# The order of TensorE's work in the FFN phases: written out from the second turned chunk on, with two edits at the first and the last chunks

## The chip, the cores and the metric

The kernel runs on one core of a Trainium2 chip. The metric is the device time of one execution in microseconds, a median of several runs. A profiled execution gives the rows below; times in them are counted from the start of its span. TensorE (PE) multiplies, VectorE (DVE) and ScalarE (ACT) work beside it, GpSimd (POOL) does little here, SyncE (SP) issues nearly all DMAs. Each engine takes its instructions in the order of its own queue and waits at semaphores for others.

## The reference

Two layers of a streaming encoder over 256 tokens of 1024 values. Each layer has a half-step FFN, a mixer (four heads of differential attention beside four mLSTM heads) and a second half-step FFN, each between two RMS norms:

```python
def _swiglu(h, w_in, w_out):
    gate, up = jnp.split(h @ w_in, 2, axis=-1)
    return (jax.nn.silu(gate) * up) @ w_out
...
for l in range(DEPTH):
    g = norm_gains[l]
    h = _swiglu(_rmsnorm(x, g[0]), ffn_w_in[l, 0], ffn_w_out[l, 0])
    x = x + 0.5 * _rmsnorm(h, g[1])
    ...
    x = x + _rmsnorm(h, g[3])
    h = _swiglu(_rmsnorm(x, g[4]), ffn_w_in[l, 1], ffn_w_out[l, 1])
    x = x + 0.5 * _rmsnorm(h, g[5])
```

D_FF is 2816, in float32. The change is in the FFN alone; the mixer's code is untouched.

## The kernel before

**Phases and chunks.** Six phases run one after the other: FFN, mixer, FFN, FFN, mixer, FFN, numbered 0 to 5. An FFN is cut into 11 chunks of 256 hidden columns. A chunk needs two weight pieces of 1 MB for its gate and up columns and a third for its rows of the out matrix.

**Weights.** `piece` (L274, L280) has SyncE load a piece into `wr` (three buffers); per half of it ScalarE makes the high part `wh` by a cast (L287) and VectorE the low part `wl` by a subtraction (L288, a "split" in what follows). A product in full precision is three matmuls: high by high, high by low, low by high (`mm3`, L400 to L402). The buffers of `wl` and `wh` come back when the last matmul that reads them is done, and a split into a buffer waits for that matmul.

**Straight and turned chunks.** In a straight chunk the tokens are the stationary operand: per token block one bank, 24 products, then silu, product and two transposes on TensorE (L536). A turned chunk has the weights stationary (`in_turned`, L603): 32 matmuls of 512 columns with the high parts (L609) and 32 of 256 columns with the low parts (L614), into four banks, two of the pool `pin` and two of the pool `ptr`, of two banks each. So each chunk takes the banks of the chunk before it. A bank is emptied in `ffn_block` (L560): ScalarE copies one half (L567), VectorE adds the other to it (L568, the last reader of the bank), multiplies by the token scales (L569), then silu, product (L572), and the parts `hh` (ScalarE, L545) and `hl` (VectorE, L546) for the out products.

**Out products.** `out_part` multiplies the hidden block of an earlier chunk by its out rows into four banks `bk`, 12 matmuls per token block. They wait in a list `pend` and are taken two chunks late; the last ones follow the last chunk.

**What sets the order.** The kernel is written as one program; a scheduler distributes it to the engines and orders each engine's queue by a simulated run, with what was written earlier first among what is ready. Inside a `manual_schedule` region the named engine keeps the written order. In `run` (L486) TensorE enters such a region at the step "ending", when the last chunk's in matrices are done, and leaves it at "running" in the next FFN; so the mixers and the starts of the FFNs are in written order, chunks 2 to 10 are not. VectorE, ScalarE and SyncE are always ordered by the scheduler.

The names in what follows are the tiles' own: `pin`, `ptr`, `bk` are banks, `both` the normalised tokens (high and low parts), `su` the emptied banks, `c` a table of constants.

Of the kernel before, what the change touches and what calls it, by code (L numbers as in the profile page):

```python
# [24 lines left out]
P = 128  # L25
D = 1024
S = 256
NT = S // P
L = 2
DFF = 2816  # L30
NC_FF = DFF // 256
# [2 lines left out]
EPS = 1e-6  # L34
BIG = -1.0e30
DEFER = 3
TURN = 2
AHEAD = 2
AT = (0, 2, 6, 6, 7, 22, 24, 24, 24, 24, 36, 40, 24, 46, 34, 50, 43, 52, 52, 57, 61, 60, 61, 67, 67, 69, 71, 78, 74, 74, 78, 84)
FIRST = """W6 V3 T000 T001 A000 A001 B000 B001 W1 V1 T002 T003 H00 L00 A002 A003 B002 B003 W1 V1 M000 H01 L01  # L40
# [90 lines left out]
class _Trunk:  # L131
# [354 lines left out]
    def run(self, phases):  # L486
        xT, r, last = [], [], []

        def enter(t, ph):
            xT.append(self.prenorm(t, ph))  # L490
            last.append(self.last)

        region = contextlib.ExitStack()
        post = []
        for ph in range(phases):
            half = ph % 3 != 1
            now = (xT, r)
            seen = 0
            self.turns = [[], [], [], [], last[:1], post] if ph else []
            for step in (self.ffn if half else self.mixer)(now, ph):  # L500
                if step == "second":
                    enter(1, ph)
                    r.append(self.rstd(1))
                    self.turns = [last[1:]] * 6
                elif step == "running":
                    region.close()
                elif step == "middle":
                    if ph == 0:
                        self.constants_mix()
                elif step == "ending":  # L510
                    region.enter_context(self.tc.manual_schedule(engines={mybir.EngineType.PE}))
                elif step == "next":
                    if ph + 1 < phases:
                        xT, r, last = [], [], []
                        enter(0, ph + 1)
                else:
                    post = [self.postnorm(seen, step[1], step[2], half, ph + 1 == phases)]
                    seen += 1
                    if seen == NT and ph + 1 < phases:
                        r.append(self.rstd(0))  # L520
        region.close()
# [66 lines left out]
    def ffn(self, pre, gi_post):  # L588
        xT, r = pre

        def in_piece(t, kh, pin, w):
            xh, xl = xT[t][kh]
            for k in range(4):
                self.mm3(pin, xh[:, k, :], xl[:, k, :], *self.cols(w, k),
                         start=kh == 0 and k == 0, stop=kh == 1 and k == 3)
# [4 lines left out]
                    self.mm3(po[t][hf], *h[t][k], *self.cols(wo, 2 * k + hf),  # L600
                             start=c == 0 and k == 0, stop=c == NC_FF - 1 and k == 1)

        def in_turned(banks, w, both):  # L603

            blocks = [(banks[j][i], slice(i * 256 + j * P, i * 256 + j * P + P)) for j in range(2) for i in range(2)]
            for kh in range(2):
                for b, c in blocks:
                    for k in range(4):
                        self.nc.tensor.matmul(b, self.cols(w[kh], k)[0][:, c], both[kh][:, k].rearrange("p i t -> p (i t)"),  # L609
                                              start=kh == 0 and k == 0, stop=False, skip_group_check=True)  # L610
            for b, c in blocks:
                for kh in range(2):
                    for k in range(4):
                        self.nc.tensor.matmul(b[:, 0:NT * P], self.cols(w[kh], k)[1][:, c], both[kh][:, k, 0:NT].rearrange("p i t -> p (i t)"),  # L614
                                              start=False, stop=kh == 1 and k == 3, skip_group_check=True)

        po, pend = None, []
        if not xT:

            xT += [[], []]  # L620
            pins = [self.bank_bk() for _ in range(NT)]
# [10 lines left out]
            begin = 1  # L632
# [29 lines left out]
        for c in range(begin, NC_FF):  # L662
            ws = [self.piece(), self.piece()]
            pend.append((c - 1, h, self.piece()))
            if c == 3:
                g = self.load_gpost(gi_post)
                yield "middle"
            if c < TURN:
                pins = [self.bank_pin() for _ in range(NT)]
                for kh in range(2):  # L670
                    for t in range(NT):
                        in_piece(t, kh, pins[t], ws[kh])
                h = [self.ffn_evac(pins[t], r[t]) for t in range(NT)]
            else:
                if c == TURN:
                    rows, both = self.token_scales(r), list(self.both)
                banks = [[self.bank_pin() for _ in range(2)], [self.bank_tr() for _ in range(2)]]
                in_turned(banks, ws, both)
                if c == NC_FF - 1:
                    break  # L680
                h = self.ffn_turned(banks, rows, c > NC_FF - DEFER - 1)
            if len(pend) == DEFER - 1 or po is None:
                if po is None:
                    po = [[self.bank_bk() for _ in range(2)] for _ in range(NT)]
                cc, hc, wo = pend.pop(0)
                for t in range(NT):
                    out_part(cc, t, hc, wo)

        yield "ending"
        pend.append((c, self.ffn_turned(banks, rows, True), self.piece()))  # L690
        for p in pend:
            out_part(p[0], 0, *p[1:])
# [562 lines left out]
```

## Time and profile before

| | us |
|---|---|
| median of three runs | 978.14 |
| the runs | 980.10, 976.82, 978.14 |
| the profiled execution | 980.56 |
| its span | 978.7 |
| TensorE busy | 967.0 (99% of the span) |
| VectorE busy | 692.4 (71%) |
| ScalarE busy | 564.4 (58%) |

The granted clock of TensorE over the span is 0.997 of full speed. Busy time is what an engine spent in instructions; TensorE's matmuls overlap by some tenths of a microsecond, so the distance between two starts tells more than the length of one. A run of 16 matmuls in one row gives the spacing by the start of the row behind it.

### The profile page before, as it was taken

Reading aid. Unit: us, or ns where it says so; the run is one execution under the profiler, and the core shown is the slowest. Engines: PE = TensorE matmul, PEld = TensorE weight load, DVE = VectorE, ACT = ScalarE, POOL = GpSimd, SP = SyncE. Lnnn points to the kernel's source line nnn. Section 1 sums busy time; section 2 is a strip of 40 time slices with the busy share of each in tenths; the row PEclk is TensorE's granted clock in tenths of the full one; section 3 lists DMA queues with packets and bytes.
Section 4 is the critical chain, followed back from the end, with each engine's and each line's share of the span. In section 5 each row is a group of like instructions: output and inputs, shape, how many; then the busy total and the mean of one; then the engine's idle time right before and its main releaser. Section 6 shows DMA issues by size and latency. Waiting matters only on the chain.

```text
span 978.7 us, 13455 instructions
## 1 busy us (share of the span) xinstructions
PE 967.0 (99%) x5067; PEld 820.0 (84%) x5067; DVE 692.4 (71%) x1177; ACT 564.4 (58%) x1041; POOL 30.0 (3%) x55
## 2 busy tenths in 40 slices
PE   9999999899999999999999999999999999999997
PEld 7888888788788888888788888888888888888886
DVE  7686667589867766857686684767898586676764
ACT  7755455378765555555375554555779475545542
POOL 2000000000020000000000000000001100000000
PEclk9999999999999999999999999999999999999999
DMA  8954546235352835464445545462464346545421
GB/s 321 337 195 169 209 159 230 115 130 196 128 215 87 310 142 214 173 215 156 189 167 204 210 173 213 156 233 90 169 234 150 111 180 232 211 170 218 152 107 44
DMA packets 27648, 178.94 MB, mean 183 GB/s; under 512 B 3034, under 2 KB 4186, under 8 KB 6846
## 3 DMA queue, kind: packets, MB, share of 16 engines
q1 hardware_dynamic: 27006, 177.46, 49.2%
q8 instruction: 40, 0.66, 0.3%
q10 hardware_dynamic: 576, 0.61, 0.2%
q14 instruction: 26, 0.21, 0.1%
HBM read 177.01 MB, written 1.05 MB: 182 GB/s over the span
## 4 chain that ended last, share of the span: by engine, by line
PE 88%; DVE 5%; DMA 4%; ACT 2%; issue 1%; DVEq 0%; POOLq 0%; ACTq 0%; SPq 0%
PE pin L609 11%; PE ptr L609 11%; PE bk L400 8%; PE bk L401 8%; PE bk L402 8%; PE pin L400 7%; PE pin L402 7%; PE pin L401 7%; PE pin L614 6%; PE ptr L614 6%; DMA wr<-in_w_dram 4%; DVE wl L288 3%; ACT wh L287 1%; PE ptr L877 1%; PE ptr L426 1%
## 5 line engine op out<-in xcount | busy, mean ns | idle before, releaser
L288 DVE TENSOR_TENSOR wl<-wr,wh 128x1024 fp32r<-128x1024 f32 x324 | 385.2, 1219 | 92.0 <-ACT wh L287 42.9
L287 ACT ACTIVATE wh<-wr 128x1024 fp32r<-128x1024 f32 x324 | 328.6, 1052 | 134.4 <-PE bk L402 38.4
L400 PE MATMUL bk<-wh,hh 128*128 128x512 f32 x352 | 138.7, 394 | 4.7 <-ACT hh L545 4.7
L609 PE MATMUL pin<-both,wh 128*128 128x512 f32 x576 | 142.5, 390 | 0.0
L609 PE MATMUL ptr<-both,wh 128*128 128x512 f32 x576 | 140.9, 389 | 0.0
L401 PE MATMUL bk<-wl,hh 128*128 128x512 f32 x352 | 138.2, 393 | 0.0
L402 PE MATMUL bk<-wh,hl 128*128 128x512 f32 x352 | 136.9, 391 | 0.0
L609 PEld LDWEIGHTS ptr<-both,wh 128*128 128x128 f32 x576 | 107.7, 188 | 22.2
L609 PEld LDWEIGHTS pin<-both,wh 128*128 128x128 f32 x576 | 107.3, 188 | 21.8
L400 PE MATMUL pin<-wh,both 128*128 128x512 f32 x304 | 122.4, 404 | 0.0
L401 PE MATMUL pin<-wl,both 128*128 128x512 f32 x304 | 119.1, 392 | 0.0
L402 PE MATMUL pin<-wh,both 128*128 128x512 f32 x304 | 118.8, 391 | 0.0
L568 DVE TENSOR_TENSOR su<-pin,su 128x256 f32<-128x256 f32 x72 | 29.2, 420 | 100.9 <-ACT su L567 100.3
L400 PEld LDWEIGHTS bk<-wh,hh 128*128 128x128 f32 x352 | 66.6, 189 | 18.4 <-ACT hh L545 5.8
L545 ACT ACTIVATE hh<-su 128x256 fp32r<-128x256 f32 (+1 forms) x96 | 32.2, 358 | 82.9 <-DVE su L572 60.3
L402 PEld LDWEIGHTS bk<-wh,hl 128*128 128x128 f32 x352 | 66.5, 189 | 14.5 <-DVE hl L546 0.5
L614 PEld LDWEIGHTS pin<-both,wl 128*128 128x128 f32 x576 | 75.5, 191 | 3.8
L614 PE MATMUL pin<-both,wl 128*128 128x256 f32 x576 | 77.1, 283 | 0.0
L401 PEld LDWEIGHTS bk<-wl,hh 128*128 128x128 f32 x352 | 66.6, 189 | 12.1
L614 PE MATMUL ptr<-both,wl 128*128 128x256 f32 x576 | 74.9, 283 | 0.0
L614 PEld LDWEIGHTS ptr<-both,wl 128*128 128x128 f32 x576 | 72.2, 192 | 0.8
L402 PEld LDWEIGHTS pin<-wh,both 128*128 128x128 f32 x304 | 57.1, 188 | 12.4
(202 smaller groups left out, 1000.5 us busy)
## 6 DMA issues: line engine op xcount, KB each, us to landing
wr<-in_w_dram SPq DMA_DIRECT2D x162, 1024.0 KB, 4.9
gpost<-in_gpost_dram SPq DMA_DIRECT2D x6, 512.0 KB, 6.0
wr<-in_w_dram SPq DMA_DIRECT2D x2, 512.0 KB, 6.0
wr<-in_w_dram SPq DMA_DIRECT2D x3, 256.0 KB, 4.2
x<-in_x_dram SPq DMA_DIRECT2D x3, 256.0 KB, 4.7
out_dram<-x SPq DMA_DIRECT2D x2, 256.0 KB, 2.2
x<-in_x_dram SPq DMA_DIRECT2D x2, 128.0 KB, 2.7
wr<-in_w_dram ACTq DMA_DIRECT2D x1, 256.0 KB, 3.2
```

The source lines that it names most:

```text
L287: ia = nc.scalar.activation(hi, raw[:, j], AF.Copy)
L288: iv = nc.vector.tensor_tensor(lo, raw[:, j], hi.bitcast(F32), op=ALU.subtract)
L400: mm(ps, xh, wh, start=start, stop=False)
L401: mm(ps, xh, wl, start=False, stop=False)
L402: mm(ps, xl, wh, start=False, stop=stop)
L426: nc.tensor.transpose(ptr[:, k, :], x[:, (4 * hf + k) * P:(4 * hf + k + 1) * P], self.ident)
L545: self.nc.scalar.activation(hh, h, AF.Copy)
L568: nc.vector.tensor_tensor(su[:, i], bank[i][:, 0:n], su[:, i], op=ALU.add)
L609: self.nc.tensor.matmul(b, self.cols(w[kh], k)[0][:, c], both[kh][:, k].rearrange("p i t -> p (i t)"), start=kh == 0 and k == 0, stop=Fals ...
L614: self.nc.tensor.matmul(b[:, 0:NT * P], self.cols(w[kh], k)[1][:, c], both[kh][:, k, 0:NT].rearrange("p i t -> p (i t)"), start=False, sto ...
L877: self.T(ptr[:, b, :], a[:, b * P:(b + 1) * P], self.tr.ident)
```

## The change

It does three things, all in the FFN.

First, TensorE's written order now begins at a step "steady", at the chunk after the first turned one (chunk 2 of phase 0, chunk 3 of the other FFNs), instead of at "ending". The out products are put in the program one by one for that: the first block of the first pending chunk after the first turned chunk, the second after the next, and from then on whole ones.

Second, chunk 1 of phase 0, straight before, is turned (TURN is gone). The row of token scales is made at the first turned chunk.

Third, `in_turned` takes the last chunk in three groups: the first weight half, high and low parts, for all four banks; then the second half for the two pin banks; then for the two ptr banks. Other chunks keep their order: all high parts, then all low parts, bank by bank.

```diff
--- before.py
+++ after.py
@@ -34,7 +34,6 @@
 EPS = 1e-6
 BIG = -1.0e30
 DEFER = 3
-TURN = 2
 AHEAD = 2
...
@@ -507,7 +506,7 @@
                 elif step == "middle":
                     if ph == 0:
                         self.constants_mix()
-                elif step == "ending":
+                elif step == "steady":
                     region.enter_context(self.tc.manual_schedule(engines={mybir.EngineType.PE}))
                 elif step == "next":
                     if ph + 1 < phases:
@@ -600,19 +599,21 @@
                     self.mm3(po[t][hf], *h[t][k], *self.cols(wo, 2 * k + hf),
                              start=c == 0 and k == 0, stop=c == NC_FF - 1 and k == 1)
 
-        def in_turned(banks, w, both):
+        def in_turned(banks, w, both, last):
+
 
             blocks = [(banks[j][i], slice(i * 256 + j * P, i * 256 + j * P + P)) for j in range(2) for i in range(2)]
-            for kh in range(2):
-                for b, c in blocks:
-                    for k in range(4):
-                        self.nc.tensor.matmul(b, self.cols(w[kh], k)[0][:, c], both[kh][:, k].rearrange("p i t -> p (i t)"),
-                                              start=kh == 0 and k == 0, stop=False, skip_group_check=True)
-            for b, c in blocks:
-                for kh in range(2):
-                    for k in range(4):
-                        self.nc.tensor.matmul(b[:, 0:NT * P], self.cols(w[kh], k)[1][:, c], both[kh][:, k, 0:NT].rearrange("p i t -> p (i t)"),
-                                              start=False, stop=kh == 1 and k == 3, skip_group_check=True)
+            for group, khs in ((blocks, (0,)), (blocks[:2], (1,)), (blocks[2:], (1,))) if last else ((blocks, (0, 1)),):
+                for kh in khs:
+                    for b, c in group:
+                        for k in range(4):
+                            self.nc.tensor.matmul(b, self.cols(w[kh], k)[0][:, c], both[kh][:, k].rearrange("p i t -> p (i t)"),
+                                                  start=kh == 0 and k == 0, stop=False, skip_group_check=True)
+                for b, c in group:
+                    for kh in khs:
+                        for k in range(4):
+                            self.nc.tensor.matmul(b[:, 0:NT * P], self.cols(w[kh], k)[1][:, c], both[kh][:, k, 0:NT].rearrange("p i t -> p (i t)"),
+                                                  start=False, stop=kh == 1 and k == 3, skip_group_check=True)
 
         po, pend = None, []
         if not xT:
@@ -665,28 +666,23 @@
             if c == 3:
                 g = self.load_gpost(gi_post)
                 yield "middle"
-            if c < TURN:
-                pins = [self.bank_pin() for _ in range(NT)]
-                for kh in range(2):
-                    for t in range(NT):
-                        in_piece(t, kh, pins[t], ws[kh])
-                h = [self.ffn_evac(pins[t], r[t]) for t in range(NT)]
-            else:
-                if c == TURN:
-                    rows, both = self.token_scales(r), list(self.both)
-                banks = [[self.bank_pin() for _ in range(2)], [self.bank_tr() for _ in range(2)]]
-                in_turned(banks, ws, both)
-                if c == NC_FF - 1:
-                    break
-                h = self.ffn_turned(banks, rows, c > NC_FF - DEFER - 1)
-            if len(pend) == DEFER - 1 or po is None:
-                if po is None:
-                    po = [[self.bank_bk() for _ in range(2)] for _ in range(NT)]
-                cc, hc, wo = pend.pop(0)
-                for t in range(NT):
-                    out_part(cc, t, hc, wo)
-
-        yield "ending"
+            if c == begin + 1:
+                yield "steady"
+            if c == begin:
+                rows, both = self.token_scales(r), list(self.both)
+            banks = [[self.bank_pin() for _ in range(2)], [self.bank_tr() for _ in range(2)]]
+            in_turned(banks, ws, both, c == NC_FF - 1)
+            if c == NC_FF - 1:
+                break
+            h = self.ffn_turned(banks, rows, c > NC_FF - DEFER - 1)
+            if po is None:
+                po = [[self.bank_bk() for _ in range(2)] for _ in range(NT)]
+
+            for t in ((0,) if c == begin else (1,) if c == begin + 1 else range(NT)):
+                out_part(pend[0][0], t, *pend[0][1:])
+            if c > begin:
+                pend.pop(0)
+
         pend.append((c, self.ffn_turned(banks, rows, True), self.piece()))
         for p in pend:
             out_part(p[0], 0, *p[1:])
```

The lines of the changed kernel are one less than before's down to in_turned (the add that empties a bank is L567, the split L287), and high and low matmuls of a turned chunk are L610 and L615.

**TensorE, from one turned chunk to the next, in phase 0.** Before, from the last low matmuls of chunk 2 into its second ptr bank (ptr_475) on; pin_649 and pin_650 are the banks of chunk 3, wh the high parts of its pieces:

```order
L614 MATMUL ptr_475<-both_187,wl_1_453 128x256 x2
L609 MATMUL pin_649<-both_129,wh_0_569 128x512 x2
L609 MATMUL pin_649<-both_129,wh_1_573 128x512 x2
L609 MATMUL pin_650<-both_129,wh_0_569 128x512 x2
L609 MATMUL pin_650<-both_129,wh_1_573 128x512 x2
L609 MATMUL pin_649<-both_187,wh_0_579 128x512 x2
L609 MATMUL pin_649<-both_187,wh_1_583 128x512 x2
L609 MATMUL pin_650<-both_187,wh_0_579 128x512 x2
L609 MATMUL pin_650<-both_187,wh_1_583 128x512 x2
```

After these rows come the low matmuls of the two pin banks and 12 out products, and then the ptr banks of chunk 3 (ptr_651, ptr_652). In the changed kernel, at the same step from chunk 1 to chunk 2, from the last low matmuls into ptr_345 on; ptr_486 and ptr_487 are the ptr banks of chunk 2, and ptr_487 is the place of ptr_345:

```order
L615 MATMUL ptr_345<-both_187,wl_1_323 128x256 x2
L610 MATMUL ptr_486<-both_129,wh_0_455 128x512 x2
L610 MATMUL ptr_486<-both_129,wh_1_459 128x512 x2
L610 MATMUL ptr_487<-both_129,wh_0_455 128x512 x2
L610 MATMUL ptr_487<-both_129,wh_1_459 128x512 x2
```

The 16 high and 16 low matmuls of the pin banks and the 12 out products no longer stand between a ptr bank's last matmul and the first of its successor; four matmuls do.

**VectorE at the same place of the changed kernel.** ptr_344 and ptr_345 are chunk 1's ptr banks, wl_0_474 to wl_1_596 the splits of two later pieces:

```order
L567 TENSOR_TENSOR su_425<-ptr_344,su_425 128x256
L568 TENSOR_TENSOR su_425<-su_425,rows_340 128x256
L545 TENSOR_TENSOR hl_411<-su_414,hh_410 128x256
L287 TENSOR_TENSOR wl_0_474<-wr_472,wh_0_475 128x1024
L287 TENSOR_TENSOR wl_1_478<-wr_472,wh_1_479 128x1024
L287 TENSOR_TENSOR wl_0_592<-wr_590,wh_0_593 128x1024
L287 TENSOR_TENSOR wl_1_596<-wr_590,wh_1_597 128x1024
L567 TENSOR_TENSOR su_425<-ptr_345,su_425 128x256
```

Each of the four splits waits for low matmuls into ptr_345, the add of ptr_345 behind them for the last of these. In the kernel before, four splits stand ahead of the two ptr adds of chunk 2 in the same way, so this order on VectorE has stayed.

**VectorE at the end of phase 0.** Before; su_1767 comes from the pin banks of the last chunk, su_1780 from its ptr banks (1695, 1696):

```order
L568 TENSOR_TENSOR su_1767<-pin_1693,su_1767 128x256
L568 TENSOR_TENSOR su_1767<-pin_1694,su_1767 128x256
L569 TENSOR_TENSOR su_1767<-su_1767,rows_470 128x256
L288 TENSOR_TENSOR wl_0_1946<-wr_1944,wh_0_1947 128x1024
L569 TENSOR_TENSOR su_1767<-su_1767,rows_470 128x256
L568 TENSOR_TENSOR su_1780<-ptr_1695,su_1780 128x256
L288 TENSOR_TENSOR wl_0_1936<-wr_1934,wh_0_1937 128x1024
L288 TENSOR_TENSOR wl_1_1940<-wr_1934,wh_1_1941 128x1024
L288 TENSOR_TENSOR wl_1_1950<-wr_1944,wh_1_1951 128x1024
L568 TENSOR_TENSOR su_1780<-ptr_1696,su_1780 128x256
L572 TENSOR_TENSOR su_1767<-su_1767 128x256
L569 TENSOR_TENSOR su_1780<-su_1780,rows_470 128x256 x2
```

And in the changed kernel, where su_1789 comes from the pin banks (1717, 1718), su_1802 from the ptr banks (1719, 1720):

```order
L287 TENSOR_TENSOR wl_0_1958<-wr_1956,wh_0_1959 128x1024
L287 TENSOR_TENSOR wl_0_1968<-wr_1966,wh_0_1969 128x1024
L567 TENSOR_TENSOR su_1789<-pin_1717,su_1789 128x256
L567 TENSOR_TENSOR su_1789<-pin_1718,su_1789 128x256
L568 TENSOR_TENSOR su_1789<-su_1789,rows_340 128x256 x2
L287 TENSOR_TENSOR wl_1_1962<-wr_1956,wh_1_1963 128x1024
L571 TENSOR_TENSOR su_1789<-su_1789 128x256
L287 TENSOR_TENSOR wl_1_1972<-wr_1966,wh_1_1973 128x1024
L567 TENSOR_TENSOR su_1802<-ptr_1719,su_1802 128x256
L567 TENSOR_TENSOR su_1802<-ptr_1720,su_1802 128x256
L545 TENSOR_TENSOR hl_1786<-su_1789,hh_1785 128x128
L568 TENSOR_TENSOR su_1802<-su_1802,rows_340 128x256 x2
```

The three splits that stood in one run ahead of the last ptr add have moved: two are ahead of the pin adds, the others single between the products.

## Rows read from the trace of the kernel before

**Rows 1.** The page, busy time, share of the span and instructions of TensorE.

```profile
PE 967.0 (99%) x5067; PEld 820.0 (84%) x5067; DVE 692.4 (71%) x1177; ACT 564.4 (58%) x1041; POOL 30.0 (3%) x55
```

**Rows 2.** What TensorE waited for in the whole span: us in total, times, the longest.

```profile
PE bk L400 <- ACT hh L545: 4.7, 3, 2.7
PE bk L389 <- PEq L1245: 0.8, 1, 0.8
```

**Rows 3.** Windows of 20 us at the ends of phases 0, 2 and 3: length, busy time of each engine (and instructions), the granted clock of TensorE as a share of full speed, DMA share, GB/s.

```profile
180.00:200.00 20.00, 17.05 (x71) 13.69 (x72) 12.61 (x25) 8.19 (x21) 1.12 (x2) 0.91 0.28 106
...
480.00:500.00 20.00, 18.49 (x89) 15.29 (x90) 13.63 (x29) 10.13 (x26) 2.14 (x4) 1.00 0.31 110
660.00:680.00 20.00, 20.00 (x99) 16.83 (x98) 15.06 (x29) 9.19 (x23) 0.55 (x1) 1.00 0.30 106
```

**Rows 4.** Timeline of TensorE at the end of phase 0: start, length, engine, line, operation, out<-in, shape, count, and in brackets the idle time before it with what ended it.

```profile
174.21 0.40 PE L400 MATMUL bk<-wh,hh 128*128 128x512 f32 x1
...
179.45 0.39 PE L402 MATMUL bk<-wh,hl 128*128 128x512 f32 x1
182.57 0.50 PE L400 MATMUL bk<-wh,hh 128*128 128x512 f32 x1 [2.73 <-ACT hh L545]
...
183.92 0.67 PE L400 MATMUL bk<-wh,hh 128*128 128x512 f32 x1 [0.38 <-ACT hh L545]
```

**Rows 5.** The window behind phase 0's second pause: length, TensorE's busy time (and matmuls), granted clock, DMA share, GB/s.

```profile
183.92:187.37 3.45, 3.45 (x8) 0.52 0.88 361
```

**Rows 6.** Timeline of VectorE at the end of phase 0.

```profile
177.96 3.48 DVE L288 TENSOR_TENSOR wl<-wr,wh 128x1024 fp32r<-128x1024 f32 x3
181.36 0.42 DVE L568 TENSOR_TENSOR su<-ptr,su 128x256 f32<-128x256 f32 x1
...
182.03 0.75 DVE L569 TENSOR_TENSOR su<-su,rows 128x256 f32<-128x256 f32 x2
...
183.90 0.29 DVE L546 TENSOR_TENSOR hl<-su,hh 128x128 fp32r<-128x128 f32 x1 [0.38 <-ACT hh L545]
```

**Rows 7.** Timeline of ScalarE at the end of phase 0.

```profile
171.90 2.95 ACT L287 ACTIVATE wh<-wr 128x1024 fp32r<-128x1024 f32 x3 [3.16 <-DMA wr<-in_w_dram]
...
182.20 0.51 ACT L545 ACTIVATE hh<-su 128x128 fp32r<-128x128 f32 x2 [5.25 <-DVE su L572]
```

**Rows 8.** Timeline of TensorE at the end of phase 2.

```profile
479.56 0.39 PE L402 MATMUL bk<-wh,hl 128*128 128x512 f32 x1
481.51 0.50 PE L400 MATMUL bk<-wh,hh 128*128 128x512 f32 x1 [1.57 <-ACT hh L545]
```

**Rows 9.** Timeline of VectorE at the end of phase 2.

```profile
474.77 2.35 DVE L288 TENSOR_TENSOR wl<-wr,wh 128x1024 fp32r<-128x1024 f32 x2
...
477.71 2.35 DVE L288 TENSOR_TENSOR wl<-wr,wh 128x1024 fp32r<-128x1024 f32 x2
479.98 0.41 DVE L568 TENSOR_TENSOR su<-ptr,su 128x256 f32<-128x256 f32 x1
```

**Rows 10.** Timeline of TensorE over the chunks 2 and 3 of phase 0, and behind the second dots of phase 2.

```profile
47.52 2.08 PE L614 MATMUL ptr<-both,wl 128*128 128x256 f32 x16
49.43 3.82 PE L609 MATMUL pin<-both,wh 128*128 128x512 f32 x16
53.09 2.08 PE L614 MATMUL pin<-both,wl 128*128 128x256 f32 x16
55.00 0.40 PE L401 MATMUL bk<-wl,hh 128*128 128x512 f32 x1
...
57.75 3.79 PE L609 MATMUL ptr<-both,wh 128*128 128x512 f32 x16
61.38 0.88 PE L614 MATMUL ptr<-both,wl 128*128 128x256 f32 x6
...
347.36 2.08 PE L614 MATMUL ptr<-both,wl 128*128 128x256 f32 x16
349.27 2.91 PE L609 MATMUL pin<-both,wh 128*128 128x512 f32 x12
```

**Rows 11.** Timeline of TensorE around one pair of transposes (L536) in the stream of matmuls, in phase 2.

```profile
331.27 0.39 PE L400 MATMUL pin<-wh,both 128*128 128x512 f32 x1
331.50 0.38 PE L536 MATMUL ptr<-c,h 128*128 128x128 f32 x2
331.63 0.47 PE L401 MATMUL pin<-wl,both 128*128 128x512 f32 x1
331.95 0.40 PE L402 MATMUL pin<-wh,both 128*128 128x512 f32 x1
```

**Rows 12.** Timeline of VectorE over the chunks 2 and 3 of phase 0.

```profile
48.97 4.63 DVE L288 TENSOR_TENSOR wl<-wr,wh 128x1024 fp32r<-128x1024 f32 x4 [4.01 <-PE ptr L614]
53.52 0.75 DVE L568 TENSOR_TENSOR su<-ptr,su 128x256 f32<-128x256 f32 x2
```

**Rows 13.** Timeline of VectorE over the chunks 2 and 3 of phase 2.

```profile
348.81 4.63 DVE L288 TENSOR_TENSOR wl<-wr,wh 128x1024 fp32r<-128x1024 f32 x4 [3.37 <-PE ptr L614]
353.36 0.75 DVE L568 TENSOR_TENSOR su<-ptr,su 128x256 f32<-128x256 f32 x2
```

**Rows 14.** DMA issues between 30 and 50 us: out<-in, queue, count, KB each, median us from issue to landing.

```profile
c<-in_c_dram SPq DMA_DIRECT2D x1, 222.0 KB, 7.4
```

**Rows 15.** The page's costliest groups, the cast of a weight half: busy, mean ns of one, idle before and what ended most of it.

```profile
L287 ACT ACTIVATE wh<-wr 128x1024 fp32r<-128x1024 f32 x324 | 328.6, 1052 | 134.4 <-PE bk L402 38.4
```

## The prediction

> **What bounds the kernel now.** I read the busy times first: TensorE works 967.0 us of a span of 978.7 [rows 1], so everything but TensorE's own work and its few pauses is hidden. The list of what TensorE waits for comes second: apart from the first 0.8 us the only named wait is the product of the out matrices (L400) for the cast of a hidden block, three times, 4.7 us in all [rows 2]. The table of windows says where: TensorE is busy 17.05 of the 20 us from 180, at a mean clock of 0.91 of full; 18.49 of the 20 us from 480, at full clock; all 20 us from 660 [rows 3]. So the ends of phases 0 and 2 cost something, the end of phase 3 nothing.
>
> The timeline then prices both ends. In phase 0 the last chunk's matrices end where the out products begin, at 174.21; call this E. 24 products fill TensorE up to 179.84 (the pause of 2.73 us that ends at 182.57 begins there), then it stands those 2.73 us, does three, and stands another 0.38 [rows 4]. After that the granted clock is 0.52 from 183.92 to 187.37, the lower of its two levels (1.2 GHz of 2.4) but for the edges [rows 5]. Eight matmuls took 3.45 us there, where at full clock they take 8 x 0.2275 = 1.82 [rows 10]: another 1.63 us. Phase 0's end therefore costs 3.11 + 1.63 = 4.74 us. In phase 2 the pause is 1.57 us [rows 8], and the clock stays whole.
>
> Why these pauses? VectorE has three weight splits of together 3.48 us at 177.96, and only after them, at 181.36, the add that empties the last bank [rows 6]; the casts of the hidden block that TensorE waits for start at 182.20 [rows 7]. In phase 2 it is two pairs of splits [rows 9]. So it is VectorE's order, not its speed: an engine that takes its queue in order puts 1.16 us per split (four in 4.63 [rows 12]) in front of 0.4 us that TensorE waits for.
>
> **The change, part by part.**
>
> *Last chunk in groups.* The pin banks now end with the ptr banks' second half still to do: 8 x 0.2275 + 8 x 0.1195 = 2.78 us ahead of E instead of 16 x 0.1195 = 1.91 [rows 10], and the first half's low parts are given back earlier. In the new order of VectorE at phase 0's end two splits precede the pin adds, and the other two stand one by one between the products. Worked from E: the piece that the second split needs landed at 171.90 = E-2.3 [rows 7]; what frees its buffer isn't moved, so I keep that. Cast 1.05 to E-1.3, split to E-0.1, two adds and two products by the token scales 1.45 to 1.35, split to 2.5, product 0.35 to 2.85, split to 4.0, two adds to 4.75, a low part of 0.29, two products to 5.75, one more to 6.1, cast of the block 0.3 to 6.4 [rows 6, 7, 12]. TensorE wants it after 24 + 3 products, 5.63 + 0.68 = 6.31. So 0.1 to 0.5 us stay; I take 0.3, and no low clock. **Gain 4.4** (bounds 0, were the landing 3 us later, and 4.7). In phase 2 the same regrouping takes the pause of 1.57 away but for some hundredths: **gain 1.5** (bounds 0 and 1.6). Phases 3 and 5 have no pause to lose: 0.
>
> *Phase 0's chunk 1 turned.* 48 matmuls of 512 columns, 10.92 us, become 32 of 512 and 32 of 256, 7.28 + 3.82 = 11.10; four transposes go, in two pairs that each take about 0.22 us out of the stream (0.13 before the next matmul, 0.09 behind its start) [rows 10, 11]. **Gain 0.25**.
>
> *TensorE in written order from the second turned chunk on.* Here the price lies. Before, the order was made by a scheduler that put a chunk's pin banks and half an out part ahead of its ptr banks: in phase 0 the low matmuls of one chunk's ptr banks end at 49.43, and the next chunk's ptr banks begin at 57.75, 8.3 us later [rows 10]. VectorE needs these: four splits from 48.97, whose buffers those very low matmuls free, then the two ptr adds from 53.52 on, done at 54.27, 4.1 to 4.8 us after the matmuls' end [rows 12, 10]. TensorE never noticed. The written order takes all four banks in a row with their first half, so the ptr banks are wanted much sooner, while the order on VectorE keeps the four splits ahead of the adds:
>
> Phase 0, chunk 1 to 2. Between the last low matmul of ptr_345 and the first matmul into its successor ptr_487 stand four matmuls, 0.91 us; on VectorE four splits and then the add of ptr_345. By [rows 12] that add is done about 4.5 us after the low matmuls. Stall 4.5 - 0.9 = **3.6** (bounds 2.7, if the splits run from the first low matmul on, and 4.3). Queued behind the waiting matmul is all of TensorE's chunk; behind the add only VectorE's own chain, with work to spare.
>
> The clock after it: 2.73 and 0.38 us idle brought 1.63 us of loss [rows 4, 5], 1.57 brought none [rows 8, 3]. 3.6 lies beyond the one that lost: **1.6** (bounds 0 and 1.75).
>
> Phase 0, chunk 2 to 3. TensorE has 12 out products and 12 matmuls, 5.5 us, before the second ptr bank, VectorE four splits, two adds and a product, 5.4: even. But a table of constants that ScalarE and VectorE handle before this chunk's copies is loaded behind the weight pieces on the sync queue, and takes 7.4 us from issue to landing [rows 14]; behind it on ScalarE wait two casts of 1.05 [rows 15] and the copies out of the pin banks. If it lands some 7 us after the split that lets the queue go on, the copies are about 1 us late, and with them the add: **1.0** (bounds 0 and 3.3).
>
> Phase 2, chunk 2 to 3. Before: low matmuls to 349.27, four splits from 348.81, adds 353.36 to 354.03 [rows 10, 13], the ptr banks again only after pins and outs. Now three out products (0.68) and eight pin matmuls (1.82) are the only cover, 2.5 of 4.5: **2.0** (bounds 1.0 and 2.4). Chunk 3 to 4: two casts that wait for their piece stand ahead of the pin copies on ScalarE; 0 to 1.0, I take **0.5**. Phase 3's chunk 2 to 3 has nine out products and eight pin matmuls, 3.87 against 4.5: **0.6** (bounds 0 and 0.7). In phase 5 the adds stand behind two splits, 0, and from the fourth chunk on 24 out products, 5.45 us, cover them everywhere: 0, for as long as the adds stand behind no more than four splits.
>
> **Sum.** -4.4 - 1.5 - 0.25 + 3.6 + 1.6 + 1.0 + 2.0 + 0.5 + 0.6 = **+3.15 us**. The profiled execution took 980.56, so it would take 983.7. That execution stands 2.4 above the median of the runs, 978.14, which themselves reach from 976.82 to 980.1. On the median the forecast is **981.3 us**.
>
> **A rule on the clock.** The row: the granted clock stayed whole over 1.57 us of idle and was 0.52 after 2.73 and 0.38 [rows 3, 5, 8]. The Trainium skill, "TensorE: Matmul & The Clock Gate", section "Why this matters for your kernels", advises against idle gaps between bursts of matmuls, since the clock then returns to the lower level. This speaks against a change that replaces two pauses by five; the trace agrees for the long one only.
>
> **Rivals.**
>
> *The follow-on stalls don't come (same).* The stall of 3.6 us at phase 0's chunk 2 gives the loads, the casts and the splits that much lead, so that the next chunk finds everything ready; likewise in phase 2. Place: phase 0 chunk 3, phase 2 chunk 4. Price: the 1.0 and 0.5 fall away, +1.65: 979.8. It decides if the table of constants lands before the pin banks are complete. For it: TensorE is never kept by a weight piece in the trace of before [rows 2], so the loads have a lead already. Against: VectorE's queue is as long as before. If also the clock stays whole, the sum is +0.05, 978.2.
>
> *No new bank wait of weight (faster).* The adds come in time, because the order that the chip meets at the ptr banks is not what I read, or the splits start on buffers that are free earlier. Place: phase 0 chunk 2 and phase 2 chunk 3; if neither waits, the end gains stand alone: 978.14 - 6.15 = 972.0; with half the stall at phase 0 and no low clock, 973.8. It decides from under 3 us of all new stalls on. Against: the splits wait for low matmuls that are the bank's own last ones, and VectorE takes them in order [rows 12].
>
> *The low clock in phase 2 too (slower).* Two us of idle lie between 1.57 and 3.1; if they suffice, another 1.6: 982.9.
>
> *The ends don't heal (slower; the change doesn't do what it says).* The chain at phase 0's end begins with a landing at E-2.3 [rows 7]; each us later is a us of pause, and from 2 us on the low clock comes back. With 3 us the gain of 4.4 is gone: 985.7.
>
> **How the numbers follow.** Chances: my forecast 0.33, the low clock in phase 2 0.08, the ends not healed 0.08, no follow-on stalls 0.36, no bank wait 0.15. A measurement of this kernel tells 0.3%, 2.9 us, from no change, so faster means under 975.2 and slower over 981.1. The forecast lies hardly beyond that line, so some of it falls to same; some of "no follow-on stalls" with a longer wait falls to slower. Faster 0.15, same 0.38, slower 0.47. The range leaves out a tenth on either side: 974.0 to 985.5; the forecast's own is 979.5 to 984.
>
> **What would show it.** In the profile of the changed kernel TensorE should wait for VectorE's add (L567) at the ptr banks: once some 3.6 us near 36 to 39 us, with granted clock near a half right after, once about 2 us in phase 2's third chunk, and under 1 us in phase 3's. The wait for the cast of the hidden block (L544) should fall from 4.7 us to under 1, and the clock in the 20 us after phase 0's end be whole. The prediction is wrong if the waits for the add sum to under 3 us, if no low clock follows the first, or if the two ends keep more than 1 us.

## The result and the profile after

The changed kernel takes 982.46 us (median of 4 runs, 982.15 to 982.90) against 977.48 for the kernel before (976.69 to 980.10), a ratio of 1.0049 with an interval of 1.0033 to 1.0065: 5.0 us slower, where +3.15 and 981.3 were forecast. The 977.48 are the three runs that the prediction started from (median 978.14) and a fourth; against 978.14 it is 4.3. The profiled execution took 982.26 with a span of 980.5.

The list of what TensorE waits for, in the changed kernel, answers to [rows 2]:

```profile
PE ptr L610 <- DVE su L567: 6.4, 4, 3.5
PE bk L388 <- PEq L1241: 0.8, 1, 0.8
```

The wait for the cast of the hidden block is gone, and a wait at the ptr banks for the add that empties them is there, four times. TensorE's timeline shows them: idle time in brackets, two in phase 0, one each in phases 2 and 3.

```profile
34.10 1.11 PE L615 MATMUL ptr<-both,wl 128*128 128x256 f32 x8
35.06 1.09 PE L610 MATMUL ptr<-both,wh 128*128 128x512 f32 x4
39.62 2.07 PE L610 MATMUL ptr<-both,wh 128*128 128x512 f32 x4 [3.47 <-DVE su L567]
...
55.72 1.21 PE L610 MATMUL ptr<-both,wh 128*128 128x512 f32 x4 [0.55 <-DVE su L567]
...
354.52 2.14 PE L610 MATMUL ptr<-both,wh 128*128 128x512 f32 x8 [1.88 <-DVE su L567]
...
540.21 2.11 PE L610 MATMUL ptr<-both,wh 128*128 128x512 f32 x8 [0.51 <-DVE su L567]
```

VectorE at the first of them, which answers to [rows 12]: four splits, then the add.

```profile
34.59 4.63 DVE L287 TENSOR_TENSOR wl<-wr,wh 128x1024 fp32r<-128x1024 f32 x4 [1.40 <-ACT wh L286]
39.14 0.42 DVE L567 TENSOR_TENSOR su<-ptr,su 128x256 f32<-128x256 f32 x1
```

The bank's last low matmul gives way to the next matmul at 35.06, the add is done at 39.56, 4.5 us later, and four matmuls were the whole cover (what TensorE has to do in the meantime).

Windows of TensorE (length, busy time, matmuls, granted clock, DMA share, GB/s), the last two in the place of [rows 3]:

```profile
20.00:40.00 20.00, 16.53 (x90) 0.98 0.80 294
40.00:60.00 20.00, 19.45 (x95) 0.93 0.64 232
...
180.00:200.00 20.00, 20.00 (x95) 1.00 0.30 106
...
480.00:500.00 20.00, 20.00 (x94) 1.00 0.26 103
```

The ends of phases 0 and 2 are dense now and at full clock; the low clock now comes around 40 us, behind the first of the four waits.

### The profile page after: what moved, and what is told of

Its sections match the earlier page's. It is cut to its first block, busy times and chain, and to the rows that moved or that the text cites. A ratio compares the mean times of both kernels' runs of the same rounds, so it can differ in the third digit from the quotient of the medians.

```text
span 980.5 us, 13501 instructions
## 1 busy us (share of the span) xinstructions
PE 967.0 (99%) x5079; PEld 819.8 (84%) x5079; DVE 697.9 (71%) x1185; ACT 566.5 (58%) x1045; POOL 29.9 (3%) x55
## 4 chain that ended last, share of the span: by engine, by line
PE 97%; DVE 2%; issue 1%; ACT 0%; POOLq 0%; DVEq 0%; ACTq 0%
PE ptr L610 14%; PE pin L610 13%; PE bk L399 10%; PE bk L400 9%; PE bk L401 9%; PE ptr L615 7%; PE pin L615 7%; PE pin L399 7%; PE pin L401 7%; PE pin L400 7%; DVE wl L287 1%; PE ptr L873 1%; PE ptr L425 1%; PE bk L1088 1%; PE bk L1126 1%
## 5 line engine op out<-in xcount | busy, mean ns | idle before, releaser
L287 DVE TENSOR_TENSOR wl<-wr,wh 128x1024 fp32r<-128x1024 f32 x324 | 386.8, 1220 | 62.5 <-ACT wh L286 37.8
L610 PE MATMUL ptr<-both,wh 128*128 128x512 f32 x592 | 147.8, 392 | 6.4 <-DVE su L567 6.4
L610 PE MATMUL pin<-both,wh 128*128 128x512 f32 x592 | 147.7, 391 | 0.0
L610 PEld LDWEIGHTS ptr<-both,wh 128*128 128x128 f32 x592 | 110.7, 189 | 31.2 <-DVE su L567 8.6
L610 PEld LDWEIGHTS pin<-both,wh 128*128 128x128 f32 x592 | 111.1, 189 | 23.1
L399 PE MATMUL pin<-wh,both 128*128 128x512 f32 x288 | 116.4, 404 | 0.0
L400 PE MATMUL pin<-wl,both 128*128 128x512 f32 x288 | 112.7, 391 | 0.0
L401 PE MATMUL pin<-wh,both 128*128 128x512 f32 x288 | 112.6, 391 | 0.0
L567 DVE TENSOR_TENSOR su<-pin,su 128x256 f32<-128x256 f32 x74 | 30.1, 421 | 101.8 <-ACT su L566 101.3
L615 PEld LDWEIGHTS pin<-both,wl 128*128 128x128 f32 x592 | 76.8, 191 | 3.5
L615 PE MATMUL pin<-both,wl 128*128 128x256 f32 x592 | 77.9, 283 | 0.0
L615 PE MATMUL ptr<-both,wl 128*128 128x256 f32 x592 | 77.8, 283 | 0.0
L615 PEld LDWEIGHTS ptr<-both,wl 128*128 128x128 f32 x592 | 74.6, 192 | 0.7
L401 PEld LDWEIGHTS pin<-wh,both 128*128 128x128 f32 x288 | 54.1, 188 | 11.8
```

The costliest lines, as they stand in the source:

```text
L287: iv = nc.vector.tensor_tensor(lo, raw[:, j], hi.bitcast(F32), op=ALU.subtract)
L399: mm(ps, xh, wh, start=start, stop=False)
L400: mm(ps, xh, wl, start=False, stop=False)
L401: mm(ps, xl, wh, start=False, stop=stop)
L567: nc.vector.tensor_tensor(su[:, i], bank[i][:, 0:n], su[:, i], op=ALU.add)
```

## Experiments

### A second profile of the kernel before

No edit.

> The kernel before, unchanged, for a second profile. Theory (the ends of phases 0 and 2 always cost what the first profile shows): TensorE waits about 4.7 us for the cast of the hidden block, and the clock is low for some 3.5 us after phase 0's end, in a span of about 978.7. Rival (the first profile, 980.56 us against a median of 977.5, fell on an execution with a longer pause or a low clock that most executions don't have): pauses of 2 to 4 us, the clock whole, and a span of about 975 to 976.5.

Measured: 978.57 us (977.20 to 980.57, 12 runs), ratio to before 1.0006 (0.9995 to 1.0017), span 977.0, 1.7 less than in the first profile. Its waits; ScalarE and TensorE at phase 0's end; the pause of phase 2; and a window of 1 us at phase 0's end (length, busy time, matmuls, granted clock, DMA share, GB/s):

```profile
PE bk L400 <- ACT hh L545: 3.2, 3, 2.1
```

```profile
170.98 2.95 ACT L287 ACTIVATE wh<-wr 128x1024 fp32r<-128x1024 f32 x3 [2.15 <-DMA wr<-in_w_dram]
```

```profile
181.65 0.50 PE L400 MATMUL bk<-wh,hh 128*128 128x512 f32 x1 [2.13 <-ACT hh L545]
...
183.00 0.50 PE L400 MATMUL bk<-wh,hh 128*128 128x512 f32 x1 [0.37 <-ACT hh L545]
```

```profile
479.75 0.50 PE L400 MATMUL bk<-wh,hh 128*128 128x512 f32 x1 [0.70 <-ACT hh L545]
```

```profile
184.00:185.00 1.00, 1.00 (x4) 0.50 0.96 401
```

3.2 us of pauses in place of 4.7: between the theory and the rival. In these two profiles the pause of phase 0 follows the landing: here the 24 products began at 181.65 - 2.13 - 5.63 = 173.89, and the casts that wait for the piece at 170.98, 2.91 us ahead; in the first profile it was 174.21 - 171.90 = 2.31 ahead [rows 4, 7]. 0.60 us earlier, and the pause 0.60 shorter. The clock fell here too, to 0.50. So the ends cost something in both executions, but not the same.

How often the clock falls there, the runs of the kernel before suggest (53 beside the experiments and these 12, each with its mean granted clock). In 20 of them it is 0.997, as in both profiles; they took 978.59 to 981.70 us, median 979.3. In the other 45 it is 0.998 or more; they took 975.77 to 978.97, median 977.1. Of the profiles of this case 0.997 stands only at those with one fall ahead of the last phase's end, so most executions of the kernel before seem to have no fall there, and both profiles show one that has. (One profile with a fall, of another kernel below, has 0.998, so a few of the 45 may have one too.)

### The last chunk's groups alone

```diff
-        def in_turned(banks, w, both):
+        def in_turned(banks, w, both, last):
...
-                in_turned(banks, ws, both)
+                in_turned(banks, ws, both, c == NC_FF - 1)
```

(with the body of the changed kernel's `in_turned`; all else as before)

> The kernel before with the last chunk's groups alone. Theory: the end pauses go as in the changed kernel, 4.7 us of idle and, where the clock fell, 1.6 more: 4.5 to 6 us faster than before, a ratio of 0.994 to 0.9955. Rival (the pauses are mostly gone in ordinary executions): 2 to 4 us faster, 0.996 to 0.998. Third (the groups need TensorE's written order to help): no gain, ratio 1.000.

Measured: 974.02 us (973.38 to 974.61) against 977.26, ratio 0.9961 (0.9946 to 0.9975). All pauses at the ends are gone from the profile and the clock is whole there, yet the gain is 3.2 us, the rival's. Windows at the ends of phases 0 and 2:

```profile
172.00:192.00 20.00, 20.00 (x101) 1.00 0.38 138
...
470.00:490.00 20.00, 20.00 (x96) 1.00 0.30 106
```

The kernel before scatters over 975.97 to 980.23 in the 23 runs of this comparison, the 6 of this one over 1.2 us: what scattered was mostly the ends.

### The written order and the turned chunk without the groups

```diff
-            in_turned(banks, ws, both, c == NC_FF - 1)
+            in_turned(banks, ws, both, False)
```

> The changed kernel without the last chunk's groups: the written order and the turned chunk alone. Theory (bank waits of 6.4 us and 1.6 of low clock are added, nothing is gained at the ends): 9 to 11 us slower than before, ratio 1.009 to 1.011, with the same four waits at the ptr banks and again about 4 us at the ends. Rival (the written order itself mends the ends): as the changed kernel, 1.005.

Measured: 985.90 us (985.75 to 987.60), ratio 1.0088 (1.0073 to 1.0103), 8.6 us slower than before, where 9 to 11 were expected. Its waits:

```profile
PE ptr L610 <- DVE su L567: 6.3, 4, 3.5
PE bk L399 <- ACT hh L544: 2.4, 3, 1.4
```

The same four waits at the banks, and 2.4 us at the ends again (about 4 were expected). The clock fell twice here: behind phase 0's first wait, where four matmuls take 1.85 us (1.20 in the second profile of the changed kernel, where the clock stays whole), and behind phase 2's, 1.88 us as in the changed kernel's first profile:

```profile
40.01 1.85 PE L610 MATMUL ptr<-both,wh 128*128 128x512 f32 x4 [3.46 <-DVE su L567]
```

```profile
18.00:62.00 44.00, 40.11 (x206) 0.96 0.72 263
...
358.00:359.00 1.00, 1.00 (x4) 0.50 0.94 385
```

The sizes add up: 8.6 for the order less 3.2 for the groups is 5.4, measured 5.0. In part that is luck: the order has two falls of the clock here (all five runs have a mean clock of 0.995 or 0.996) and one in each profile of the changed kernel, while the ends without the groups keep 2.4 us and no fall.

### The splits behind the add

```diff
+            if begin < c <= begin + 2:
+                a = [(None, self.add)]
+                self.turns = self.turns[:2] + [[]] * (4 - len(self.turns[:2])) + [a] * 4
...
-            nc.vector.tensor_tensor(su[:, i], bank[i][:, 0:n], su[:, i], op=ALU.add)
+            self.add = nc.vector.tensor_tensor(su[:, i], bank[i][:, 0:n], su[:, i], op=ALU.add)
```

> The changed kernel with VectorE's order told: in the two chunks after the first turned one of each FFN, the splits of the third piece and of the next chunk's first piece come behind the add that empties the last bank. TensorE's order stays. Theory (VectorE's order alone makes the bank waits): the waits at the ptr banks fall from 6.4 to under 1 us, the clock stays whole, 7 to 8 us faster than the changed kernel, 974 to 975.5, 2 to 3.5 faster than before. Rival (the splits are late in their turn, and TensorE waits for weights instead, or the banks are needed before any order of VectorE can give them): no more than 3 us faster than the changed kernel.

Measured: 976.10 us (974.71 to 977.61), ratio to before 0.9984 (0.9975 to 0.9993): 6.4 faster than the changed kernel, where 7 to 8 were expected. Three of the four waits are gone; phase 0's first is 1.97 us, not under 1. Here are TensorE, VectorE and ScalarE at that place:

```profile
37.93 1.61 PE L610 MATMUL ptr<-both,wh 128*128 128x512 f32 x4 [1.97 <-DVE su L567]
```

```profile
37.45 0.42 DVE L567 TENSOR_TENSOR su<-ptr,su 128x256 f32<-128x256 f32 x1 [3.72 <-ACT su L566]
```

```profile
35.16 1.99 ACT L286 ACTIVATE wh<-wr 128x1024 fp32r<-128x1024 f32 x2
37.06 0.36 ACT L566 ACTIVATE su<-ptr 128x256 f32<-128x256 f32 x1
```

VectorE stands idle for 3.72 us in front of the add: it waits for ScalarE's copy, and that stands behind two casts. In the changed kernel the copy began at the same 37.06, hidden under the splits. And the clock fell behind this wait, as a window of 1 us shows (length, busy time, matmuls, granted clock, DMA share, GB/s):

```profile
39.00:40.00 1.00, 1.00 (x4) 0.50 0.00 0
```

### The casts behind the copy as well

```diff
-                a = [(None, self.add)]
+                a = [(self.copy, self.add)]
...
-            nc.scalar.activation(su[:, i], bank[i][:, n:2 * n], AF.Copy)
+            self.copy = nc.scalar.activation(su[:, i], bank[i][:, n:2 * n], AF.Copy)
```

> The kernel adds_first with ScalarE told as well: the casts of the same pieces come behind the copy out of the last bank. Theory (two queues in turn hold the bank back, VectorE's splits and, behind them, two casts of 1.05 us on ScalarE): the one wait left, 1.97 us at phase 0's second turned chunk, falls to 0.2 to 0.5, the clock stays whole, 3 to 3.5 us faster than adds_first: 972.5 to 973.5, ratio to before 0.995 to 0.9965. Rival (casts and splits that come later hold up TensorE for a weight part, or a load): no more than 1.5 us faster than adds_first, with new waits for wh or wl.

Measured: 973.35 us (973.03 to 974.31), ratio to before 0.9959 (0.9945 to 0.9973), 9.1 faster than the changed kernel (8.7 when each is set against the kernel before that ran beside it) and 2.75 faster than the last experiment, a little less than the 3 to 3.5 expected. TensorE, ScalarE and VectorE:

```profile
35.14 2.29 PE L610 MATMUL ptr<-both,wh 128*128 128x512 f32 x8
37.27 1.98 PE L610 MATMUL pin<-both,wh 128*128 128x512 f32 x8
```

```profile
35.34 0.38 ACT L566 ACTIVATE su<-ptr 128x256 f32<-128x256 f32 x1 [1.75 <-PE ptr L615]
35.62 4.84 ACT L286 ACTIVATE wh<-wr 128x1024 fp32r<-128x1024 f32 x5
```

```profile
35.76 0.42 DVE L567 TENSOR_TENSOR su<-ptr,su 128x256 f32<-128x256 f32 x1 [2.28 <-ACT su L566]
```

Eight matmuls into the ptr banks from 35.14 to 37.27, where eight take 1.82 at full clock: 0.3 us left of the wait. TensorE's order is that of the changed kernel, matmul for matmul. This version beats both kernels.

### Turned chunk and groups, TensorE's order as before

```diff
-            if c == begin + 1:
-                yield "steady"
...
+        yield "steady"
         pend.append((c, self.ffn_turned(banks, rows, True), self.piece()))
```

> The changed kernel with the written order of TensorE from the last chunk on only, as before: the groups and phase 0's turned chunk 1 without the new order. Theory (the written order alone makes the bank waits; turning chunk 1 gains 0.25 us by itself): 0.3 us beside ends_only, 973.5 to 974.5, and no waits at the ptr banks over 0.5 us. Rival (turning chunk 1 makes phase 0's wait, in either order): 3 to 5 us slower than ends_only.

Measured: 973.71 us (972.99 to 974.83), ratio to before 0.9961 (0.9948 to 0.9974). No wait at a ptr bank; the largest left beside the start is 0.35 us, at the end of phase 3:

```profile
660.66 0.50 PE L401 MATMUL bk<-wh,hl 128*128 128x512 f32 x1 [0.35 <-DVE hl L545]
```

So the written order alone makes the changed kernel slow, 982.46 - 973.71 = 8.75 us, or 8.3 when each is set against the kernel before that ran beside it. The 0.3 us to the groups alone (0.1 in the same way) fit the price of the turned chunk, and are less than either kernel scatters.

### The written order one chunk later

```diff
-            if c == begin + 1:
+            if c == begin + 2:
                 yield "steady"
```

> The changed kernel with the written order one chunk later (chunk 3 of phase 0, chunk 4 of the others). Theory (a wait at a ptr bank is the time until the add, some 4.5 us, less the matmuls that stand between, and one chunk later 12 or 24 out products stand there): phase 0's wait of 3.5 us and its low clock go, phase 2's 1.9 and phase 3's 0.5 go, at most about 0.5 us stays in phase 0: 974 to 975.5, 7 to 8.5 us faster than the changed kernel. Rival (the first chunk in written order always pays, whichever it is): within 3 us of the changed kernel, with the long wait one chunk later.

Measured: 977.66 us (976.93 to 978.51), ratio to before 0.9999 (0.9988 to 1.0011): 4.8 faster than the changed kernel, where the theory had 7 to 8.5. Phase 0 is free of waits; its waits, and TensorE and VectorE in phase 2:

```profile
PE pin L610 <- DVE su L567: 1.5, 3, 0.7
PE ptr L610 <- DVE su L567: 1.2, 1, 1.2
```

```profile
357.94 0.40 PE L399 MATMUL bk<-wh,hh 128*128 128x512 f32 x1
...
359.32 1.98 PE L610 MATMUL pin<-both,wh 128*128 128x512 f32 x8
362.49 2.11 PE L610 MATMUL ptr<-both,wh 128*128 128x512 f32 x8 [1.19 <-DVE su L567]
```

```profile
357.47 4.63 DVE L287 TENSOR_TENSOR wl<-wr,wh 128x1024 fp32r<-128x1024 f32 x4 [3.22 <-PE ptr L615]
362.02 0.75 DVE L567 TENSOR_TENSOR su<-ptr,su 128x256 f32<-128x256 f32 x2
```

The add is done 4.5 us after the low matmuls' end at 357.94, as forecast; but only six out products and eight pin matmuls stand between, 1.38 + 1.82 = 3.2, since the scheduler took the other six ahead of the ptr banks. The rule held, my count of the cover did not. The three waits at pin banks are in phases 3 and 5 (0.74, 0.51, 0.28); the theory had none there. In phase 3 four splits stand ahead of an add once more, of a pin bank this time:

```profile
542.41 4.63 DVE L287 TENSOR_TENSOR wl<-wr,wh 128x1024 fp32r<-128x1024 f32 x4 [4.50 <-PE ptr L615]
546.95 0.42 DVE L567 TENSOR_TENSOR su<-pin,su 128x256 f32<-128x256 f32 x1
```

All bank waits together are 2.7 us; this kernel is 3.95 slower than the one with TensorE's order as before (973.71), and what makes the rest is open.

### The ends mended by the order of two queues alone

```diff
-            self.turns = [[], [], [], [], last[:1], post] if ph else []
+            self.turns = [self.tail] * 4 + [last[:1], post] if ph else []
+            self.tail = []
...
-        self.nc.scalar.activation(hh, h, AF.Copy)
-        self.nc.vector.tensor_tensor(hl, h, hh.bitcast(F32), op=ALU.subtract)
+        ia = self.nc.scalar.activation(hh, h, AF.Copy)
+        iv = self.nc.vector.tensor_tensor(hl, h, hh.bitcast(F32), op=ALU.subtract)
+        self.tail = [(ia, iv)]
```

> The kernel before with TensorE's order and the last chunk as they are; only the casts and splits of the next phase's first two pieces come behind the last chunk's whole chain on ScalarE and VectorE. Theory (the end pauses are VectorE's order, and the last chunk's groups help by letting splits go ahead of the chain and between it): the pauses of phases 0 and 2 go and the gain is that of ends_only, 3 to 3.5 us, ratio 0.996 to 0.9970. Rival (the late pieces, not the order, set the ends): the pauses move to the next phase's first matmuls, which wait for wh or wl there; less than 1.5 us gained, or a loss.

Measured: 974.75 us (974.54 to 975.77) against 978.23, ratio 0.9966 (0.9953 to 0.9979), 3.5 us faster. TensorE runs the order of before and waits for nothing but the first instruction:

```profile
PE bk L390 <- PEq L1248: 0.8, 1, 0.8
```

So the end pauses were the order on VectorE and ScalarE. The prediction named VectorE alone; the edit moves ScalarE's casts as well, and does not tell the two apart. In the trace of before both have a part. VectorE's first add at phase 0's end waits for ScalarE's copy, which stands behind the three casts of [rows 7], and VectorE's own three splits [rows 6] come after it:

```profile
175.15 0.76 DVE L568 TENSOR_TENSOR su<-pin,su 128x256 f32<-128x256 f32 x2 [7.58 <-ACT su L567]
```

### A second profile of the changed kernel

No edit.

> The changed kernel once more, for a second profile. Theory (its waits come from the order of two queues and not from when loads land): the four waits at the ptr banks within 0.2 us of 3.47, 0.55, 1.88 and 0.51. Open by any theory: whether the clock falls behind the 1.88 us of phase 2, as it did in no_groups at the same place, or stays whole, as in the first profile; a fall would add some 1.6 us.

Measured: 984.12 us, one run. The waits are 3.46, 1.74, 1.88 and 0.52; the second is not within 0.2 of 0.55. TensorE at that place, and windows behind the first and the third wait:

```profile
56.13 1.19 PE L610 MATMUL ptr<-both,wh 128*128 128x512 f32 x4 [1.74 <-DVE su L567]
```

```profile
354.89:360.26 5.37, 5.37 (x16) 0.68 0.75 313
39.96:44.84 4.88, 4.88 (x22) 1.00 1.03 356
```

The same windows in the first profile, in the other order:

```profile
39.62:43.90 4.28, 4.28 (x13) 0.64 0.98 339
354.52:358.32 3.80, 3.80 (x16) 1.00 1.03 433
```

The clock fell once in each, but at another wait. The second wait follows ScalarE, here and in the first profile, at the table of constants:

```profile
45.01 0.31 ACT L198 ACTIVATE c_wgc<-c 128x128 fp32r<-128x128 f32 x1 [1.75 <-DMA c<-in_c_dram]
```

```profile
44.60 0.31 ACT L198 ACTIVATE c_wgc<-c 128x128 fp32r<-128x128 f32 x1 [1.37 <-DMA c<-in_c_dram]
```

The table lands 5.0 us after the first wait's end in both (45.01 - 39.96, 44.60 - 39.62), whatever the clock does, and TensorE's second wait ends 11.12 us after the landing in both (56.13 - 45.01, 55.72 - 44.60), as in the kernel without the groups (56.19 - 45.07). With a whole clock TensorE comes sooner and waits 1.2 us longer. So this wait does hang on a landing, against the theory. The queues have their part: between the landing and the add stand two casts on ScalarE and four splits on VectorE, and where the copies go ahead of the table, as in the experiment with the splits behind the add, the wait is gone. That the landing sets it is read from the times; no run moves the load.

## Why the prediction was right, and where it was off

**The bank waits: right.** Phase 0's first was put at 3.6 and measured 3.47, phase 2's at 2.0 and 1.88, phase 3's at 0.6 and 0.51. The working (add 4.5 us behind the low matmuls, less the matmuls between) held at each, and in the kernel with the later order. The wait put at 0.5 for phase 2's next chunk did not come. The experiments on the two queues show the cause, with one addition: hidden under VectorE's four splits stood two casts on ScalarE, which alone hold the add back to 37.45. The prediction priced the first gate and did not see the second, neither here nor at the ends.

**The wait behind the table of constants: right in kind.** Put at 1.0; 0.55 and 1.74 in two executions, each with the copies behind the load. The prediction's count for VectorE at that place, "four splits, two adds and a product, 5.4", is the length without the product; with it, it is 5.7; and its two adds of phase 2 end at 354.11, not 354.03 [rows 13]. No term of the sum hangs on either.

**The low clock: right for one profile, by luck for the other.** 1.6 us were put behind the wait of 3.6. The first profile shows it there: 12 matmuls in 4.28 us from 39.62 (the window lists 13), where 12 x 0.2275 = 2.73 are full speed, 1.55 lost. The second shows it behind the 1.88 us of phase 2: 16 matmuls in 5.37 against 3.64, 1.7 lost. The rival in which it falls in phase 2 came true in place of the forecast there, not on top of it; in the kernel without the groups it came on top. By the prediction's own sign ("if no low clock follows the first") the second profile speaks against its reading of the clock: the length of the wait alone did not decide.

**The turned chunk: not settled.** 0.25 forecast; 0.1 to 0.3 between two kernels that scatter by more.

**The ends: the mechanism right, the size off.** The pauses went fully, in the groups alone and in the changed kernel. But 4.4 + 1.5 us were put down, and the groups measure 3.2. The step that failed is the last one of the sum: "On the median the forecast is 981.3 us". The gains were read from an execution that stood 2.4 us above the median, and what put it there was, by the second profile and by the mean clock of the runs, to a good part the very pauses and the low clock that go. The 1.63 us of low clock in the 4.4 seem to be missing in most of the 65 runs. Taken against the median, 5.9 less 2.4 is 3.5, near the measured 3.2 and 3.5. With it the sum is +5.5, measured +5.0. Against the execution that it was read from the account closes: 4.7 us of pauses and 1.6 of low clock go, 6.4 of bank waits and 1.55 of low clock come, +1.65; the two spans differ by 1.8.

That the forecast is no further off than 1.85 us is in part luck. The bank waits and the low clock were put at 9.3 and are 8.0 in the first profile, so costs and gains were both put too high, and the two errors partly cancel.

Of the rivals, the one without bank waits fell with the waits; the one without follow-on waits was right for phase 2 and wrong for phase 0; the ends did heal.

From runs and profile together: groups -3.2, turned chunk -0.1 to -0.3, bank waits +6.4, low clock +1.55, in all some +4.5; measured +5.0.

## What to carry to other kernels

Before the engine that bounds a kernel is held to a written order, list for each buffer that it refills what stands in the releasing engines' queues ahead of the release, and count the work between the last use and the refill: here 4.5 us against 0.9 to 3.9. The cure was not the order of TensorE but that of the two engines that empty its banks; told to empty first, they gave some 9 us back under the very same matmul order, and the written order was then worth no more than the scheduler's. A gain read from one execution is to be set against that execution, and where that one lies above the median, some of what it shows is what puts it there. The mean clock of each run was on record here and hinted at which kind of execution had been profiled.

## What was not expected of the hardware

The clock's fall does not go by the length of the idle time alone. In these profiles it fell behind 1.88 us (the second profile of the changed kernel, and the kernel without groups at the same place) and 1.97 us (the splits behind the add), and stayed whole behind 3.46 us in the second profile of the changed kernel and behind 1.88 us in its first. The kernel without groups lost it behind both its 3.46 and its 1.88 us. What else decides it is open. Of the Trainium skill's advice against idle gaps ("TensorE: Matmul & The Clock Gate", section "Why this matters for your kernels") the traces bear out the direction, each fall having idle time ahead of it; when a gap costs a fall they don't settle.
